# Moving four pieces of the mixer's query and gate work to GpSimd and ScalarE, and joining the first input transfers, in a two-layer decoder trunk

## The chip, the cores and the metric

The kernel runs on one core of a Trainium2 chip. The metric is the time of one launch in device microseconds (us); the median over repeated runs counts. The engines go by the names that the profile uses: PE is TensorE (matmuls), DVE is VectorE, ACT is ScalarE, POOL is GpSimd, SP is SyncE (its queue issues most of the transfers).

## What is computed

A trunk of two layers over 256 tokens of width 1024, in float32. Each layer is half a feed-forward block, three token mixers side by side, and another half feed-forward block:

```python
for l in range(DEPTH):
    x = x + 0.5 * swiglu_ffn(x, ffn1_norm[l], ffn1_w_gu[l], ffn1_w_down[l])
    h = rms_norm(x, mix_norm[l])
    x = x + hybrid_mixer(h, w_in[l], w_gate[l], ...)
    x = x + 0.5 * swiglu_ffn(x, ffn2_norm[l], ffn2_w_gu[l], ffn2_w_down[l])

# in the mixer (A: stick-breaking, B: NSA, C: DSA attention)
... = jnp.split(h @ w_in, offs, axis=-1)               # all queries, keys and values
qg = apply_rope(rms_norm(q, q_norm), cos, sin)         # B: 8 query heads of 64, the norm per head
kc = rms_norm(nsa_compress(k_cmp, ...), k_norm[0])     # B: compressed keys
g_a, g_b, g_c = jnp.split(jax.nn.sigmoid(h @ w_gate), 3, axis=-1)
merged = g_a * (o_a @ w_br_a) + g_b * (o_b @ w_br_b) + g_c * (o_c @ w_br_c)
return merged @ w_out
```

The kernel has the norm of `h` in two parts: the weights of the norm are multiplied into the matmul's input `aT`, and the token's reciprocal root mean square (`R`, one number for each token) is multiplied onto what the matmul gives.

## The kernel before

**Units.** All large products are made in units of 128 rows of weights by up to 1024 columns. For each unit the SP queue fetches the weights into one of four `raw` buffers; ACT copies them into `wh`, rounded to the matmul's reduced float type (L242); DVE subtracts, `wl = raw - wh` (L244); PE multiplies with both parts (L196) and adds up in a PSUM bank. `wh` and `wl` have three buffers each, and the program puts a unit's copy and subtraction two units ahead of its matmuls (`LA = 2`). So PE needs from DVE one subtraction of 128x1024 for each unit, on time.

**Threads between the units.** The small work of the mixer stands in Python generators. After each unit `tick()` lets each generator that is due go on to its next `yield n`, which means "again after n units". `keys` splits and transposes the keys, `compress` makes the compressed keys, `indexer` makes C's scores and picks keys by a chain of MAX8 and MATCH_REPLACE8 instructions on DVE, `queries` norms and rotates B's queries. The order of the matmuls is fixed by the program; for the other engines a scheduler sets an order that is then fixed, and each engine works through its own queue in that order.

**PSUM.** There are three banks with the tag `acc`, two with `tp` (for transposes on PE, L689) and two with `sc`. A third pair of transposes has to wait until the first has been copied out.

**The names at the change.** `gl` holds the gates' product with `R`: DVE reads the PSUM bank and `R` in one instruction of 128x512 (L624, `gate_rows`). `q8[0]` and `q8[1]` (tokens 0 to 127 and 128 to 255; `q8_402` and `q8_403` in the order below) hold the eight query heads, 128x512 each: multiplied by the norm `y` (L676) and by the norm's weights `hg` (L679), rotated (`ra`, `rb`, L648 to L652), then copied to a high part on ACT (L880) and subtracted for a low part on DVE (L881), and transposed on PE. `kD` is the transposed key of branch C, copied out of a `tp` bank by `evens` (L631), which takes ACT and DVE in turn. `dq` are C's queries; their transposes are copied out into `qD` (ACT, L795). `kC` is the transposed compressed key (ACT, L869). `hrep` is the compressor's hidden layer (DVE, L843), which PE multiplies by `w2` into the bank `o`. `p` copies on ACT (L526) take the key units' sums out of the `acc` banks. `dq<-p,dq`, `kk<-p,kk` and `kc<-p,kc` on POOL are low parts of keys and of C's queries (L700, L790), and `p<-c2s,cst` (L865) is a masked copy of the compressed values.

**The opening.** `x` comes in four transfers on SP's queue, each ahead of a unit's weights; the norms' weights `gn` (48 numbers for each partition) come by a transfer of their own from ACT's queue. ACT multiplies the first two blocks of `x` by `gn` (L375) and copies the first weights, and DVE makes the low parts.

## Time and profile before

| | |
|---|---|
| median of 3 runs | 1208.97 us (1208.77 to 1208.98) |
| the profiled execution: its time | 1211.23 us |
| the profiled execution: its span | 1209.5 us |
| PE busy | 1197.8 us, 99% of the span |
| PE's weight loads (beside the matmuls) | 1070.7 us, 89% |
| DVE busy | 884.2 us, 73% |
| ACT busy | 697.9 us, 58% |
| POOL busy | 145.8 us, 12% |

The span is the stretch on the chip from the first to the last instruction of the profile; the time of that execution holds 1.7 us more around it, and is 2.3 us over the median, so the profile's microseconds are used for differences and not for the whole. PE's 99% is busy time in which matmuls run on from one to the next; the 1% beside it is the start, the end and a few waits in the middle. The busy shares of the other engines are means over the whole span, and stretches of it differ a lot from these means.

### The profile page before, as it was taken

To read this page: it belongs to the slowest core of one execution; us is meant where nothing else is said; L and a number is where in the kernel's file an instruction comes from. 1 tells how busy PE (TensorE), PEld (TensorE's weight loads), DVE (VectorE), ACT (ScalarE), POOL (GpSimd) and SP (SyncE) were. 2 spreads that over 40 slices of the span, in tenths; PEclk is the share of its full clock that TensorE was granted. 3 is DMA by queue.
4 is the path that set the end of the run, shared out by engine and by line. 5 is a ranking of instruction groups with operands and counts; after the bars stand their busy time and mean duration, and the time that the engine had idled before them with its cause. 6 is when DMAs were issued, how large, how long until landed. Compare 5 with 4: busy or idle time off the path is not lost. (4 is left out here: it accounts for less than half of the span.)

```text
span 1209.5 us, 20859 instructions
## 1 busy us (share of the span) xinstructions
PE 1197.8 (99%) x7878; PEld 1070.7 (89%) x7878; DVE 884.2 (73%) x1577; ACT 697.9 (58%) x1261; POOL 145.8 (12%) x181
## 2 busy tenths in 40 slices
PE   8999999999999999999999999999999999999998
PEld 7888888879999988888888888898898999888887
DVE  7766677897766877776777666788977587876664
ACT  6655555565675565555555555555666745655542
POOL 2211011220000111110111110112100001111100
PEclk9999999999999999999999999999999999999999
DMA  7555566644334555556656555666533345555563
GB/s 263 187 185 184 179 190 200 216 152 136 122 95 152 180 189 190 190 187 190 191 181 192 189 182 184 188 188 219 166 123 113 106 155 187 191 192 192 183 200 106
DMA packets 60885, 212.09 MB, mean 175 GB/s; under 512 B 6992, under 2 KB 8048, under 8 KB 60784
## 3 DMA queue, kind: packets, MB, share of 16 engines
q1 hardware_dynamic: 60192, 209.65, 54.2%
q0 software_dynamic: 448, 1.08, 0.4%
q8 instruction: 62, 1.02, 0.3%
q14 instruction: 39, 0.32, 0.1%
q10 hardware_dynamic: 144, 0.02, 0.0%
HBM read 209.15 MB, written 1.05 MB: 174 GB/s over the span
## 5 line engine op out<-in xcount | busy, mean ns | idle before, releaser
L242 ACT ACTIVATE wh<-raw 128x1024 fp32r<-128x1024 f32 (+4 forms) x402 | 412.2, 1028 | 401.8 <-PE acc L196 277.8
L244 DVE TENSOR_TENSOR wl<-raw,wh 128x1024 fp32r<-128x1024 f32 (+4 forms) x400 | 473.9, 1187 | 211.5 <-ACT wh L242 210.6
L196 PE MATMUL acc<-aT,wh 128*128 128x512 f32 (+1 forms) x1696 | 415.1, 343 | 1.3 <-ACT wh L242 1.3
L196 PEld LDWEIGHTS acc<-aT,wh 128*128 128x128 f32 x1696 | 265.0, 189 | 41.9 <-ACT wh L242 1.7
L196 PE MATMUL acc<-aT,wl 128*128 128x256 f32 x1280 | 297.9, 281 | 1.2 <-DVE wl L244 1.2
L196 PE MATMUL acc<-hT,wh 128*128 128x512 f32 (+1 forms) x792 | 236.2, 367 | 0.0
L196 PEld LDWEIGHTS acc<-aT,wl 128*128 128x128 f32 x1280 | 216.1, 190 | 3.7 <-DVE wl L244 2.8
L196 PE MATMUL sc<-aT,wh 128*128 128x512 f32 x544 | 191.7, 396 | 0.0
L196 PE MATMUL acc<-hT,wl 128*128 128x256 f32 x704 | 184.5, 280 | 0.0
L196 PEld LDWEIGHTS acc<-hT,wh 128*128 128x128 f32 x792 | 137.2, 188 | 25.8
L196 PE MATMUL sc<-aT,wl 128*128 128x256 f32 x544 | 151.1, 279 | 0.0
L196 PEld LDWEIGHTS acc<-hT,wl 128*128 128x128 f32 x704 | 126.8, 188 | 0.0
L196 PEld LDWEIGHTS sc<-aT,wh 128*128 128x128 f32 x544 | 101.8, 188 | 24.0
L442 POOL TENSOR_TENSOR v<-v,R 128x256 f32<-128x256 f32 x88 | 70.6, 806 | 412.3 <-DVE v L358 359.2
L196 PEld LDWEIGHTS sc<-aT,wl 128*128 128x128 f32 x544 | 102.4, 188 | 0.4
L386 POOL TENSOR_TENSOR ssum<-ssum,sq 128x256 f32<-128x256 f32 x42 | 38.3, 912 | 445.5 <-ACT sq L385 445.3
L196 PE MATMUL acc<-wh,aT 128*128 128x512 f32 (+1 forms) x320 | 81.1, 394 | 0.2
L196 PEld LDWEIGHTS acc<-wh,aT 128*128 128x128 f32 x320 | 57.5, 188 | 11.0 <-ACT p L526 1.1
L357 ACT ACTIVATE half<-acc 128x256 f32<-128x256 f32 x136 | 49.5, 366 | 3.7 <-PE acc L196 3.2
L444 DVE TENSOR_TENSOR v<-v,v 128x256 f32<-128x256 f32 x88 | 38.2, 436 | 13.3 <-ACT v L443 5.8
L358 DVE TENSOR_TENSOR v<-acc,half 128x256 f32<-128x256 f32 x108 | 44.7, 417 | 1.5 <-ACT half L357 1.5
L376 DVE SCALAR_TENSOR_TENSOR aT<-x,gn,aT 128x256 fp32r<-128x256 f32 x48 | 40.6, 856 | 7.0 <-ACT aT L375 7.0
(239 smaller groups left out, 1217.2 us busy)
## 6 DMA issues: line engine op xcount, KB each, us to landing
raw<-in_gu SPq DMA_DIRECT2D x175, 512.0 KB, 4.0
raw<-in_dn SPq DMA_DIRECT2D x64, 512.0 KB, 3.7
raw<-in_wgate SPq DMA_DIRECT2D x48, 512.0 KB, 3.6
raw<-in_win SPq DMA_DIRECT2D x32, 512.0 KB, 3.7
raw<-in_dn SPq DMA_DIRECT2D x32, 384.0 KB, 3.0
raw<-in_wbr SPq DMA_DIRECT2D x16, 512.0 KB, 3.5
raw<-in_wout SPq DMA_DIRECT2D x16, 512.0 KB, 3.5
raw<-in_cw SPq DMA_DIRECT2D x8, 512.0 KB, 4.4
```

The lines of the kernel that those rows point to most:

```text
L196: return pe(T.matmul(o, lhsT=lhsT, rhs=rhs, start=start, stop=stop, skip_group_check=True))
L242: A.activation(out=wh[:, w], in_=raw[:, w], func=AF.Copy)
L244: e.tensor_tensor(out=wl[:, w], in0=raw[:, w], in1=wh[:, w].bitcast(F32), op=ALU.subtract)
L357: A.activation(out=t, in_=b[:, S:2 * S], func=AF.Copy)
L358: V.tensor_tensor(out=o, in0=b[:, 0:S], in1=t, op=ALU.add)
L376: V.scalar_tensor_tensor(out=dst[:, m, 1], in0=xs[m], scalar=g[:, m:m + 1], in1=dst[:, m, 0].bitcast(F32), op0=ALU.mult, op1=ALU.subtract)
L386: G.tensor_tensor(out=ssum, in0=ssum, in1=sq, op=ALU.add)
L442: G.tensor_tensor(out=g, in0=g, in1=N["R"], op=ALU.mult)
L444: V.tensor_tensor(out=u, in0=u, in1=g, op=ALU.mult)
```

## The change

Six edits, in two places of the program.

In the opening: `x` and the norms' weights lie in one array and one tile, `gn` in front. The first transfer of it (the weights and two blocks of `x`) is issued from ACT's queue, the transfer of `gn` alone is gone, and SP's queue begins with the first unit's weights.

In each layer's mixer:
- the first two of the six gate groups are copied from PSUM to `gl` by ACT, and the product with `R` is made in place by POOL (`scaled`, put off by 22 units); the other groups stay on DVE;
- the queries' product with `hg` is made by POOL (`nh == 8` are B's queries);
- the queries' low part is made by POOL;
- `kD` is always copied out by ACT;
- `compress` waits three units and not two before its product with `w2`.

```diff
--- before.py
+++ after.py
@@ -121,7 +121,7 @@
 
 
 @with_exitstack
-def decoder_trunk(ctx: ExitStack, tc: tile.TileContext, x_in, consts, gains, hgain, gu1, dn1, win, wkc, wgate, cw1, cw2,
+def decoder_trunk(ctx: ExitStack, tc: tile.TileContext, x_in, consts, hgain, gu1, dn1, win, wkc, wgate, cw1, cw2,
                   cpe, wbr, wout, gu2, dn2, out, depth=DEPTH):
     nc = tc.nc
     V, A, G, T = nc.vector, nc.scalar, nc.gpsimd, nc.tensor
@@ -154,15 +154,16 @@
     def cc(name):
         return cst[:, _C[name][0]:_C[name][1]]
 
-    xt_ = cpool.tile([P, KD, S], F32, tag="x", name="x")
-    xs = [xt_[:, m] for m in range(KD)]
-    gn = cpool.tile([P, DEPTH * 3, KD], F32, tag="gn", name="gn")
-    nc.scalar.dma_start(out=gn, in_=gains.rearrange("p (a k) -> p a k", k=KD))
-    xv = x_in.rearrange("p (k s) -> p k s", s=S)
+
+    NG = DEPTH * 3 * KD
+    xt_ = cpool.tile([P, NG + KD * S], F32, tag="x", name="x")
+    xs = [xt_[:, NG + m * S:NG + (m + 1) * S] for m in range(KD)]
+    gn = xt_[:, 0:NG].rearrange("p (a k) -> p a k", k=KD)
 
     first = [wpool.tile([P, D], F32, tag="raw", bufs=RAW, name=nm("raw")) for _ in range(KD // 2)]
     for u, w in enumerate(first):
-        nc.sync.dma_start(out=xt_[:, 2 * u:2 * u + 2], in_=xv[:, 2 * u:2 * u + 2])
+        k = slice(NG + 2 * u * S if u else 0, NG + 2 * (u + 1) * S)
+        (nc.sync if u else nc.scalar).dma_start(out=xt_[:, k], in_=x_in[:, k])
         n = D if u else D // 2
         for h in range(0, D, n):
             nc.sync.dma_start(out=w[:, h:h + n], in_=gu1[0][:, u * D + h:u * D + h + n])
@@ -621,10 +622,20 @@
                     return
                 if n % 2 == 0:
                     gl[n // 2] = b4("gl")
-                V.tensor_tensor(out=gl[n // 2][:, (n % 2) * 512:(n % 2 + 1) * 512].rearrange("p (a b) -> p a b", b=S),
-                                in0=gb[n].rearrange("p (a b) -> p a b", b=S),
-                                in1=N["R"].unsqueeze(1).to_broadcast([P, 2, S]), op=ALU.mult)
+                g = gl[n // 2][:, (n % 2) * 512:(n % 2 + 1) * 512].rearrange("p (a b) -> p a b", b=S)
+                b = gb[n].rearrange("p (a b) -> p a b", b=S)
+                r = N["R"].unsqueeze(1).to_broadcast([P, 2, S])
+                if n < 2:
+
+                    A.activation(out=g, in_=b, func=AF.Copy)
+                    spawn(scaled(g, r), 22)
+                else:
+                    V.tensor_tensor(out=g, in0=b, in1=r, op=ALU.mult)
             return f
+
+        def scaled(g, r):
+            G.tensor_tensor(out=g, in0=g, in1=r, op=ALU.mult)
+            yield 1
 
         turn = [0]
 
@@ -676,7 +687,8 @@
             V.tensor_tensor(out=v, in0=v, in1=r.unsqueeze(3).to_broadcast([P, nt, nh, HD]), op=ALU.mult)
             for a, n, k in gs:
                 g = hg[:, k * HD:(k + 1) * HD].unsqueeze(1).unsqueeze(1)
-                V.tensor_tensor(out=v[:, :, a:a + n], in0=v[:, :, a:a + n], in1=g.to_broadcast([P, nt, n, HD]),
+                e = G if nh == 8 else V
+                e.tensor_tensor(out=v[:, :, a:a + n], in0=v[:, :, a:a + n], in1=g.to_broadcast([P, nt, n, HD]),
                                 op=ALU.mult)
             yield 1
             rope(v, nh, 8, tab("cs")[:, t0:t0 + nt], tab("sn")[:, t0:t0 + nt])
@@ -784,7 +796,7 @@
                     A.activation(out=kSW[:, m, :, s], in_=heads(tp), func=AF.Copy)
                 yield 1
                 tp = transposes([k1[:, 0, 0:P], k1[:, 0, P:256]])
-                evens(out=kD[:, :, s], in_=heads(tp))
+                A.activation(out=kD[:, :, s], in_=heads(tp), func=AF.Copy)
             dq = b4("dq").rearrange("p (t h a d) -> p t h a d", t=NT, a=2, d=HD)
             A.activation(out=dq[:, :, :, 0].bitcast(F32R), in_=p1[:, :, 0:4], func=AF.Copy)
             G.tensor_tensor(out=dq[:, :, :, 1], in0=p1[:, :, 0:4], in1=dq[:, :, :, 0], op=ALU.subtract)
@@ -841,7 +853,7 @@
                 a, b = (v[:, kv * 2 * NC:(kv + 1) * 2 * NC].rearrange("p (g c) -> p g c", c=NC).unsqueeze(1)
                         .to_broadcast([P, 4, 2, NC]) for v in (hs, tp))
                 V.tensor_tensor(out=hrep[:, kv, :, :, 0:NC], in0=b, in1=a, op=ALU.mult)
-            yield 2
+            yield 3
             c2 = hid[:, S + P:2 * S]
             for kv in range(2):
                 mm(c2[:, kv * HD:(kv + 1) * HD], hrep[:, kv].rearrange("p i g c -> p (i g c)"), w2[:, kv], True, True)
@@ -878,7 +890,7 @@
             yield 2
             for t in range(NT):
                 A.activation(out=q8[t][:, :, 0:HD].bitcast(F32R), in_=q8[t][:, :, HD:P], func=AF.Copy)
-                V.tensor_tensor(out=q8[t][:, :, HD:P], in0=q8[t][:, :, HD:P], in1=q8[t][:, :, 0:HD], op=ALU.subtract)
+                G.tensor_tensor(out=q8[t][:, :, HD:P], in0=q8[t][:, :, HD:P], in1=q8[t][:, :, 0:HD], op=ALU.subtract)
             yield 2
             for t in range(NT):
                 for h in range(0, 8, 4):
@@ -1233,9 +1245,9 @@
     wbr = np.concatenate([i["w_br_a"], i["w_br_c"], wb], 1).reshape(L, KD, P, 4, S).transpose(0, 2, 3, 1, 4)
     wg = i["w_gate"].reshape(L, D, 3, 4, S)[:, :, ::-1].transpose(0, 1, 3, 2, 4).reshape(L, D, 3 * D)
     return {
-        "x": np.ascontiguousarray(i["x"].reshape(S, KD, P).transpose(2, 1, 0).reshape(P, KD * S)),
+        "x": np.concatenate([gains.transpose(2, 0, 1).reshape(P, -1),
+                             i["x"].reshape(S, KD, P).transpose(2, 1, 0).reshape(P, KD * S)], 1),
         "consts": _CONST,
-        "gains": np.ascontiguousarray(gains.transpose(2, 0, 1).reshape(P, -1)),
         "hgain": np.ascontiguousarray(hg),
         "gu1": gu1, "dn1": _tiles(i["ffn1_w_down"], [P] * KD),
         "win": _tiles(i["w_in"][:, :, _in_columns()], IN_G),
```

**The order at the queries, first layer.** On POOL, from the second pair of keys' low parts (`kk_562` before, `kk_560` now) to the last low part ahead of the next weights; `kc4_564` before is the compressed key (`kc4_569` now), and `p1_565` (`p1_570` now) is the masked copy of the compressed values. Before:

```order
L700 TENSOR_TENSOR kk_562_2862<-p1_401_2152,kk_562_2862 128x4x128
L700 TENSOR_TENSOR kc4_563_2865<-p1_401_2152,kc4_563_2865 128x128
L790 TENSOR_TENSOR dq_586_2990<-p1_401_2152,dq_586_2990 128x8x64
L865 TENSOR_TENSOR p1_565_2881<-c2s_532_2752,cst_70 128x512
L700 TENSOR_TENSOR kc4_564_2878<-c2s_532_2752,kc4_564_2878 128x128
```

Now:

```order
L712 TENSOR_TENSOR kk_560_2848<-p1_401_2150,kk_560_2848 128x4x128
L712 TENSOR_TENSOR kc4_561_2851<-p1_401_2150,kc4_561_2851 128x128
L802 TENSOR_TENSOR dq_586_2988<-p1_401_2150,dq_586_2988 128x8x64
L877 TENSOR_TENSOR p1_570_2920<-c2s_549_2804,cst_70 128x512
L637 TENSOR_TENSOR gl_503_2618<-gl_503_2618,R_454_2332 128x512
L691 TENSOR_TENSOR q8_402_2151<-q8_402_2151,hg_393_2137 128x8x64
L691 TENSOR_TENSOR q8_403_2152<-q8_403_2152,hg_393_2137 128x8x64
L893 TENSOR_TENSOR q8_402_2151<-q8_402_2151 128x8x64
L712 TENSOR_TENSOR kc4_569_2917<-c2s_549_2804,kc4_569_2917 128x128
L893 TENSOR_TENSOR q8_403_2152<-q8_403_2152 128x8x64
```

Between the masked copy and the compressed key's low part stand four new instructions of 128x512, the gate's product, the two halves of the queries times `hg`, and the first half's low part; the second half's low part stands behind.

On DVE in the same place. The `wl` are weights' subtractions, `isc` rows (the key choice) don't stand here, `w` and `y` belong to norms, `c2s`, `cra` and `crb` to the compressed key. Before, from the first half's product with `hg` to the copy of `kD`:

```order
L679 TENSOR_TENSOR q8_402_2153<-q8_402_2153,hg_393_2139 128x8x64
L860 TENSOR_TENSOR c2s_532_2752<-cra_555_2821,crb_556_2822 128x16
L663 SCALAR_TENSOR_TENSOR y_553_2812<-w_554_2813,y_553_2812 128x8
L648 TENSOR_TENSOR ra_578_2956<-q8_402_2153,cst_70 128x128
L676 TENSOR_TENSOR q8_403_2154<-q8_403_2154,y_553_2812 128x8x64
L649 TENSOR_TENSOR rb_579_2957<-q8_402_2153,cst_70 128x8x8
L679 TENSOR_TENSOR q8_403_2154<-q8_403_2154,hg_393_2139 128x8x64
L650 TENSOR_TENSOR rb_579_2957<-q8_402_2153,cst_70 128x8x8
L244 TENSOR_TENSOR wl_584_2971<-raw_582_2968,wh_583_2970 128x1024
L652 TENSOR_TENSOR q8_402_2153<-ra_578_2956,rb_579_2957 128x8x16
L637 CAST kD_414_2165<-tp_585_2986 128x2x128
```

Now, from the second half's product with the norm on:

```order
L687 TENSOR_TENSOR q8_403_2152<-q8_403_2152,y_547_2799 128x8x64
L674 SCALAR_TENSOR_TENSOR y_553_2810<-w_554_2811,y_553_2810 128x1
L245 TENSOR_TENSOR wl_573_2925<-raw_571_2922,wh_572_2924 128x1024
L867 SCALAR_TENSOR_TENSOR c2s_549_2804<-c2s_549_2804,y_553_2810,hg_393_2137 128x64
L659 TENSOR_TENSOR ra_578_2954<-q8_402_2151,cst_70 128x128
L869 TENSOR_TENSOR cra_562_2870<-c2s_549_2804,cst_70 128x16
L870 TENSOR_TENSOR crb_563_2871<-c2s_549_2804,cst_70 128x8
L871 TENSOR_TENSOR crb_563_2871<-c2s_549_2804,cst_70 128x8
L660 TENSOR_TENSOR rb_579_2955<-q8_402_2151,cst_70 128x8x8
L872 TENSOR_TENSOR c2s_549_2804<-cra_562_2870,crb_563_2871 128x16
L661 TENSOR_TENSOR rb_579_2955<-q8_402_2151,cst_70 128x8x8
L245 TENSOR_TENSOR wl_584_2969<-raw_582_2966,wh_583_2968 128x1024
```

The products with `hg` and the copy of `kD` are gone; both products with the norm stand ahead of the weights' subtraction `wl_573` and of the compressed key's rows, and the first half's rotation behind them. After these rows comes the last row of the first half's rotation (`q8_402<-ra_578,rb_579`), as before.

**The order at the transposes, first layer.** On ACT; `wh` are copies of weights, `tp_585` holds `kD`'s transposes, `tp_592` those of C's first queries. Before, from the compressed key's high part on:

```order
L699 ACTIVATE kc4_564_2878<-c2s_532_2752 128x128
L880 ACTIVATE q8_402_2153<-q8_402_2153 128x8x64
L242 ACTIVATE wh_595_3029<-raw_594_3027 128x1024
L795 ACTIVATE qD_412_2163<-tp_592_3017 128x4x128
L869 ACTIVATE kC_415_2166<-tp_593_3023 128x64
L880 ACTIVATE q8_403_2154<-q8_403_2154 128x8x64
L242 ACTIVATE wh_601_3068<-raw_600_3066 128x1024
```

Now, from the first half's high part on:

```order
L892 ACTIVATE q8_402_2151<-q8_402_2151 128x8x64
L243 ACTIVATE wh_590_2999<-raw_589_2997 128x1024
L711 ACTIVATE kc4_569_2917<-c2s_549_2804 128x128
L799 ACTIVATE kD_414_2163<-tp_585_2984 128x2x128
L892 ACTIVATE q8_403_2152<-q8_403_2152 128x8x64
L243 ACTIVATE wh_594_3023<-raw_593_3021 128x1024
L807 ACTIVATE qD_412_2161<-tp_592_3015 128x4x128
L243 ACTIVATE wh_601_3066<-raw_600_3064 128x1024
```

The copy of `kD` is new on ACT and stands behind the queries' first high part, a copy of weights and the compressed key's high part; the copy to `qD` comes after the second half's high part and another copy of weights; the copy to `kC` has gone further back.

On PE in the same place; `tp` rows are transposes, `acc` rows a unit's matmuls. Before:

```order
L689 MATMUL tp_592_3017<-cst_70,dq_586_2990 128x128 x4
L689 MATMUL tp_593_3023<-cst_70,kc4_564_2878 128x128 x2
L196 MATMUL acc_574_2930<-wh_583_2970,aT_8_143 128x512 x2
L196 MATMUL acc_575_2931<-wh_583_2970,aT_8_143 128x512 x2
L196 MATMUL acc_574_2930<-wh_583_2970,aT_8_143 128x512 x2
L196 MATMUL acc_575_2931<-wh_583_2970,aT_8_143 128x512 x2
L196 MATMUL acc_574_2930<-wl_584_2971,aT_8_143 128x512 x2
L196 MATMUL acc_575_2931<-wl_584_2971,aT_8_143 128x512 x2
L689 MATMUL tp_597_3050<-cst_70,dq_586_2990 128x128 x4
L196 MATMUL acc_603_3072<-wh_590_3001,aT_8_143 128x512 x2
```

Now:

```order
L701 MATMUL tp_592_3015<-cst_70,dq_586_2988 128x128 x4
L197 MATMUL acc_574_2928<-wh_583_2968,aT_8_141 128x512 x2
L197 MATMUL acc_575_2929<-wh_583_2968,aT_8_141 128x512 x2
L197 MATMUL acc_574_2928<-wh_583_2968,aT_8_141 128x512 x2
L197 MATMUL acc_575_2929<-wh_583_2968,aT_8_141 128x512 x2
L197 MATMUL acc_574_2928<-wl_584_2969,aT_8_141 128x512 x2
L197 MATMUL acc_575_2929<-wl_584_2969,aT_8_141 128x512 x2
L701 MATMUL tp_596_3044<-cst_70,dq_586_2988 128x128 x4
L701 MATMUL tp_599_3060<-cst_70,kc4_569_2917 128x128 x2
L197 MATMUL acc_603_3070<-wh_590_2999,aT_8_141 128x512 x2
```

The compressed key's transposes (from `kc4_564` before, from `kc4_569` now) have moved from right behind the first transposes of `dq` to right behind the second ones. The `tp` bank of the second ones is that of `kD`'s transposes, and the bank of the compressed key's that of the first ones of `dq`.

## Rows read from the trace of the kernel before

**Rows 1.** The page's first part: busy time of each engine, its share of the span, and its instructions.
```profile
PE 1197.8 (99%) x7878; PEld 1070.7 (89%) x7878; DVE 884.2 (73%) x1577; ACT 697.9 (58%) x1261; POOL 145.8 (12%) x181
```

**Rows 2.** PE's waits over the whole span: what PE waited with, for what, then us in total, times, longest us.
```profile
PE tp L689 <- DVE kD L637: 2.9, 2, 1.5
PE acc L196 <- ACT wh L242: 1.3, 1, 1.3
...
PE o L196 <- ACT wh L242: 0.7, 1, 0.7
```

**Rows 3.** Busy time of each engine in two stretches, one in each layer, from the mixer's key units to its query transposes.
```profile
245.00:278.00 33.00, 30.72 (x177) 26.36 (x178) 33.00 (x99) 21.26 (x41) 5.97 (x6) 1.00 0.47 147
842.00:876.00 34.00, 32.44 (x185) 27.45 (x185) 34.00 (x102) 21.73 (x42) 6.32 (x6) 1.00 0.47 149
```

**Rows 4.** PE's timeline in the first layer: start, duration, engine, line, operation, out<-in, tiles, and in brackets the idle time ahead and what ended it.
```profile
243.92 1.07 PE L196 MATMUL acc<-wl,aT 128*128 128x512 f32 x4
245.68 0.63 PE L196 MATMUL o<-w,hrep 128*128 128x64 f32 x4 [0.70 <-ACT wh L242]
...
265.17 0.60 PE L689 MATMUL tp<-cst,dq 128*128 128x128 f32 x4
267.24 0.41 PE L689 MATMUL tp<-cst,kc 128*128 128x128 f32 x2 [1.47 <-DVE kD L637]
267.40 2.08 PE L196 MATMUL acc<-wh,aT 128*128 128x512 f32 x8
269.32 1.07 PE L196 MATMUL acc<-wl,aT 128*128 128x512 f32 x4
270.24 0.60 PE L689 MATMUL tp<-cst,dq 128*128 128x128 f32 x4
270.59 2.48 PE L196 MATMUL acc<-wh,aT 128*128 128x512 f32 x8
272.90 1.07 PE L196 MATMUL acc<-wl,aT 128*128 128x512 f32 x4
```

**Rows 5.** The same of the second layer.
```profile
862.54 0.60 PE L689 MATMUL tp<-cst,dq 128*128 128x128 f32 x4
864.60 0.41 PE L689 MATMUL tp<-cst,kc 128*128 128x128 f32 x2 [1.46 <-DVE kD L637]
...
867.98 2.47 PE L196 MATMUL acc<-wh,aT 128*128 128x512 f32 x8
```

**Rows 6.** DVE's timeline in the first layer.
```profile
245.31 0.27 DVE L843 TENSOR_TENSOR hrep<-o,hs 128x120 f32<-128x120 f32 x1
...
255.02 1.25 DVE L244 TENSOR_TENSOR wl<-raw,wh 128x1024 fp32r<-128x1024 f32 x1
...
256.26 1.26 DVE L657 TENSOR_SCALAR u<-hs 128x8 f32<-128x8 f32 x2
...
258.62 0.67 DVE L624 TENSOR_TENSOR gl<-acc,R 128x512 f32<-128x512 f32 x1
...
261.72 0.68 DVE L676 TENSOR_TENSOR q<-q,y 128x512 f32<-128x512 f32 x1
...
262.64 0.68 DVE L679 TENSOR_TENSOR q<-q,hg 128x512 f32<-128x512 f32 x1
...
264.34 0.95 DVE L679 TENSOR_TENSOR q<-q,hg 128x512 f32<-128x512 f32 x1
...
265.35 1.21 DVE L244 TENSOR_TENSOR wl<-raw,wh 128x1024 fp32r<-128x1024 f32 x1
266.48 0.28 DVE L652 TENSOR_TENSOR q<-ra,rb 128x128 f32<-128x128 f32 x1
266.68 0.41 DVE L637 CAST kD<-tp 128x256 fp32r<-128x256 f32 x1
...
269.96 1.28 DVE L881 TENSOR_TENSOR q<-q 128x512 f32<-128x512 f32 x2
```

**Rows 7.** POOL's timeline in the first layer.
```profile
253.07 1.30 POOL L700 TENSOR_TENSOR kk<-p,kk 128x512 f32<-128x512 f32 x1 [7.96 <-ACT kk L699]
...
255.24 2.18 POOL L790 TENSOR_TENSOR dq<-p,dq 128x512 f32<-128x512 f32 x1
257.50 1.05 POOL L865 TENSOR_TENSOR p<-c2s,cst 128x512 f32<-128x512 f32 x1
263.88 0.86 POOL L700 TENSOR_TENSOR kc<-c2s,kc 128x128 f32<-128x128 f32 x1 [5.33 <-ACT kc L699]
```

**Rows 8.** ACT's timeline in the first layer.
```profile
266.79 0.63 ACT L880 ACTIVATE q<-q 128x512 fp32r<-128x512 f32 x1 [2.99 <-DVE q L652]
267.33 1.04 ACT L242 ACTIVATE wh<-raw 128x1024 fp32r<-128x1024 f32 x1
268.27 0.58 ACT L795 ACTIVATE qD<-tp 128x512 fp32r<-128x512 f32 x1
...
270.54 0.46 ACT L526 ACTIVATE p<-acc,rq 128x256 f32<-128x256 f32 x1
```

**Rows 9.** The opening, all engines and queues (ACTq is ACT's queue, where transfers are issued).
```profile
0.74 0.41 ACTq L160 DMA_DIRECT2D gn<-in_gains  x1
...
5.60 0.91 ACT L375 ACTIVATE aT<-x,gn 128x256 fp32r<-128x256 f32 x2 [2.93 <-DMA gn<-in_gains]
...
6.87 0.72 PE L196 MATMUL acc<-aT,wh 128*128 128x512 f32 x2 [1.29 <-ACT wh L242]
```

## The prediction

> **What bounds the kernel now.** I read the page's first part, then PE's waits, then the two stretches that the change touches, and in these the timelines of the four engines.
>
> PE is busy for 99% of the span [rows 1]. So work taken off another engine is worth something only where PE waits for it. The list of PE's waits is short: 2.9 us in two waits for DVE's copy of `kD`, 0.7 us put down to ACT ahead of the product with `hrep`, and 1.3 us at the opening [rows 2]. The edits in the mixer can win from the first two and the few tenths beside them, no more.
>
> Why do these waits exist? In the stretch from the key units to the queries' transposes DVE is busy for 33.00 of 33.00 us in the first layer and for 34.00 of 34.00 in the second, while ACT has 21.26 and POOL 5.97 [rows 3]. There the queue of DVE sets the time, against 73% in the mean. I measure PE's waits as start minus start, since the modelled ends run into the next row:
>
> - `hrep`, first layer only: four `acc<-wl` matmuls take 0.92 (269.32 to 270.24), from 243.92 to 245.68 it is 1.76: 0.84 lost [rows 4]. It is put down to ACT, but DVE ends `hrep` at 245.58 (245.31 + 0.27) [rows 6], 0.1 ahead of PE's start: it waits for DVE.
> - The transposes of `kc`: transposes of `dq` take 0.35 (270.24 to 270.59), from 265.17 to 267.24 it is 2.07: 1.72 lost. In the second layer, 862.54 to 864.60, 1.71 [rows 4, 5]. DVE starts the copy of `kD` at 266.68 [rows 6] in a queue behind products, rotation and weights.
> - Eight `acc<-wh` matmuls last 2.48 in place of 2.08 (2.47 against 2.10 there): 0.40 and 0.37 lost [rows 4, 5]. ACT's `p` copies, which begin at 270.54 [rows 8], free a bank in their middle.
>
> Together 2.96 in the first layer and 2.08 in the second, 5.04 in all.
>
> **What DVE and POOL do to each other.** The same `q<-q,hg` on DVE takes 0.68 at 262.64 and 0.95 at 264.34 [rows 6]; from 263.88 to 264.74 POOL was at `kc` [rows 7]. Two `u` of 128x8 take 1.26 [rows 6] and end at 257.52, 0.10 after POOL's `dq` (255.24 + 2.18 = 257.42) [rows 7]. And `dq` has 2.18 where `kk` of the same size has 1.30 [rows 7]. So they hold each other up, each until the other's instruction ends, and an instruction put on POOL holds back DVE's next one that is touched by this. The chip's behaviour here decides the case.
>
> [...] By the whole of a `kk` as the block, the sum below would be some 0.9 us higher.
>
> **The change, part by part.** POOL gets six instructions of 128x512 in a layer. Price of one: from 1.05 (`p<-c2s,cst`) over 1.30 (`kk`) to 2.18 (`dq`) as elapsed time [rows 7]; once DVE lets go, `dq` ran from about 256.27 (the end of the weights' subtraction, 255.02 + 1.25 [rows 6]) to 257.42: 1.15. I take 1.15, since these too will start out of such a wait.
>
> DVE gives up, by spacing of starts: two `gl` of 0.60, two `q<-q,hg` of 0.60 and up, two low parts of 0.60 (1.28 for two), one `kD` of 0.34 [rows 6]. Of the first `gl` and the low parts nothing counts ahead of the rotation.
>
> [...]
>
> *The waits that go.* `compress` asks for `hrep` one unit later, some 2.8 us (267.40 to 270.24 is a unit [rows 4]), and DVE has it by 245.6: the 0.84 are won. The transposes of `kc` no longer need the bank of `kD`: the 1.7 go from there, but the second transposes of `dq` now need that bank, and those of `kc` the bank of the first ones.
>
> *First layer and second, on the clock of rows 4 to 8.* DVE has no idle time, so rows taken out bring on what follows, and blocks push it back.
>
> 1. First product with the norm, 261.72 before [rows 6]. Out ahead of it: `gl` 0.60, the weights' subtraction 1.13 (265.35 to 266.48), the block in `u` 1.1 (1.26 less the 0.14 or so that they need), and 0.7 for the compressed key's small rows and a MATCH_REPLACE that now stand behind (an estimate from durations of 0.07 to 0.4). In: the second half's small rows 0.2, and three blocks: `dq` 0.7, the masked copy 0.7, `gl` 0.9. These are 1.15, 1.05 and 1.15 less the 0.3 to 0.45 in which DVE has rows of the key choice, which are not held up. So 261.72 - 3.53 + 2.5 = 260.7.
> 2. The two products follow each other, 260.7 to 262.0. Then POOL's first product with `hg` holds until 263.15, and the weights' subtraction `wl_573` ends at 264.4. PE wants it at 265.17 - 0.92 = 264.25 [rows 4], in the first layer at 263.4 since 0.84 were won: waits of 1.0 and 0.15.
> 3. POOL's second product, 264.35 to 265.5, holds DVE for 1.1. Then the first half's rotation and the compressed key's rows, 1.0, the subtraction `wl_584`, 1.13, and the last row, 0.28: 267.9. Before it was 266.48 + 0.28 = 266.76.
> 4. ACT: high part 0.54 (266.79 to 267.33), weights 0.94 (267.33 to 268.27) [rows 8], the compressed key 0.25, `kD` 0.41 as on DVE [rows 6]: 270.05. PE wants the second transposes of `dq` 0.35 + 2.84 after the first, which now start near 265.35: 268.55. Wait 1.5, in both layers.
> 5. ACT: second high part, weights, `qD` (0.58 [rows 8]): 272.1. PE wants the transposes of `kc` at 270.45: wait 1.7.
> 6. ACT: weights and two `p` copies: 273.8. PE wants the bank some 0.6 after the transposes of `kc`, at 272.75: wait 1.05, where 0.4 were.
>
> Sum: 1.0 + 1.5 + 1.7 + 1.05 = 5.25 in the first layer, 0.15 + 4.25 = 4.4 in the second: 9.65 against 5.04, so +4.6 us.
>
> The first queries' transposes come 3.6 us after that (272.90 to 276.54 before), and the last low part on POOL ends some 2 us ahead of them: no term. The gates' products are wanted after 290 us: none either; without this cover the POOL price of 1.15 each.
>
> *The opening.* ACT starts `aT` at 5.60 when `gn` lands, and PE starts at 6.87 after the copy of weights [rows 9]. With `gn` in the same transfer as `x` and the weights asked for first, the two land together as before or some tenths to either side: 0, with 0.6 to both sides.
>
> Forecast: 1208.97 + 4.6 + 0 = 1213.6 us (the median; differences carry over, the profiled execution's own 1211.23 would become 1215.8).
>
> **Rivals.**
> - *Late, but absorbed (as before).* The waits 4 to 6 come from one lateness of some 2.3 us a layer: each microsecond that the first rotation is earlier takes one from the sum of its layer. If DVE is held up by only half of what I put (the blocks fall on rows of the key choice, which are let through; step 2 and 3 hold 4.5 of blocks), the sum is again 5 and the time 1209, within 2 either way. For it: the scheduler's order has such rows at hand. Against it: behind both products with the norm stands none of them.
> - *POOL doesn't hold DVE up.* Then the rotation is 4.5 earlier, `hrep` and `kD` cost nothing and only the 0.4 stay: 5.04 - 0.77 = 4.3 won, 1204.7 us. It decides from the point where `kD`'s copy ends before 268.55. Against it: the 0.95 and the 1.26 above.
> - *POOL's price is that of `dq`.* Three products in the chain with 1.0 more each, in two layers: +6, 1219.6 us. For it: 2.18 is in the rows. Against it: that time holds a wait for DVE which I have counted.
> - *The mixer's edits are neutral and only the opening shows:* 1208.4 to 1209.6; it falls in with the first rival.
>
> **How the numbers follow.** The forecast's case has 0.50, its own range is 1211.3 to 1217 (prices 1.05 to 1.30, opening 0.6, step 1 uncertain by 0.5 a layer). Absorbed: 0.25. No holding up: 0.17. `dq`'s price: 0.08. The range, 1205 to 1218, leaves out the last and about half of the third, 0.17. What counts as no change is 0.2%, 2.4 us, so 1206.6 to 1211.4. Faster: 0.17 + 0.04 of the absorbed. Same: 0.19 of the absorbed, 0.03 of the forecast's. Slower: 0.47 + 0.02 + 0.08.
>
> **What would show it.** In the list of PE's waits: `hrep` gone; `tp` waiting for ACT at the second transposes of `dq` and at `kc`, 1.5 and 1.7 in each layer. On DVE, rows of 1.2 to 1.8 us just behind the two products with the norm, that end with POOL's. On POOL, products with `hg` of 1.15 to 2. On ACT, the first high part at 267 to 268, later than 266.79. Wrong if DVE runs on at 0.68 beside POOL, or if ACT copies `kD` ahead of the high part's wait: then the forecast falls to a rival. A new wait outside these stretches is nowhere in my sum.

## The result, and the profile after

The changed kernel takes 1219.17 us (median, 1215.11 to 1219.24) against 1208.87 us before: ratio 1.0081, 95% interval 1.0068 to 1.0093. It is slower, as forecast, but by 10 us and not by 4.6, and outside the range of 1205 to 1218. The profiled executions are 1211.23 us before and 1219.24 us after, 8.0 apart; what the other 2 may be is told in the last section.

The page's first part: the span has grown from 1209.5 to 1217.5 us, PE's busy time only by 4.9 [rows 1].

```profile
PE 1202.7 (99%) x7878; PEld 1074.3 (88%) x7878; DVE 887.5 (73%) x1563; ACT 699.2 (57%) x1267; POOL 166.7 (14%) x193
```

PE's waits over the whole span (waited with, for what; us in total, times, longest):

```profile
PE tp L701 <- ACT qD L807: 3.1, 2, 1.6
PE tp L701 <- ACT kD L799: 2.2, 2, 1.1
PE acc L197 <- DVE wl L245: 1.7, 3, 0.8
PE acc L197 <- ACT p L527: 1.5, 2, 0.8
```

The wait for `kD` on DVE and the one ahead of `hrep` [rows 2] are gone; in their place PE waits for the copies of `qD` and `kD` on ACT and for a bank that ACT's `p` copies free. PE's timeline in the first layer (start, duration, ..., in brackets the idle time ahead and what ended it), to be read against [rows 4]:

```profile
247.52 0.56 PE L197 MATMUL o<-w,hrep 128*128 128x64 f32 x4
...
262.98 1.19 PE L197 MATMUL acc<-wl,aT 128*128 128x512 f32 x4 [0.43 <-DVE wl L245]
...
266.30 1.08 PE L197 MATMUL acc<-wl,aT 128*128 128x512 f32 x4
268.47 0.66 PE L701 MATMUL tp<-cst,dq 128*128 128x128 f32 x4 [1.09 <-ACT kD L799]
270.70 0.44 PE L701 MATMUL tp<-cst,kc 128*128 128x128 f32 x2 [1.57 <-ACT qD L807]
270.90 0.70 PE L197 MATMUL acc<-wh,aT 128*128 128x512 f32 x2
272.38 2.92 PE L197 MATMUL acc<-wh,aT 128*128 128x512 f32 x6 [0.78 <-ACT p L527]
275.10 1.42 PE L197 MATMUL acc<-wl,aT 128*128 128x512 f32 x4
```

And in the second [rows 5]:

```profile
864.64 1.20 PE L197 MATMUL acc<-wl,aT 128*128 128x512 f32 x4 [0.47 <-DVE wl L245]
...
870.14 0.66 PE L701 MATMUL tp<-cst,dq 128*128 128x128 f32 x4 [1.09 <-ACT kD L799]
872.37 0.44 PE L701 MATMUL tp<-cst,kc 128*128 128x128 f32 x2 [1.57 <-ACT qD L807]
...
874.04 2.93 PE L197 MATMUL acc<-wh,aT 128*128 128x512 f32 x6 [0.77 <-ACT p L527]
```

By starts, as the prediction measured it, the first layer loses 0.6 for the weights' low part `wl`, 1.25 at the second transposes of `dq` (268.47 - 266.30 - 0.92), 1.88 at those of `kc` (270.70 - 268.47 - 0.35) and 1.0 at the bank (272.38 - 270.90 - 0.47 for two matmuls): 4.7. The second layer has 0.6, 1.26, 1.88 and 1.0. Together 9.5 against 5.04 before: +4.4.

Then something that was not in my sum. Six `acc<-wh` matmuls from 272.38 to 275.10 take 2.72, where eight took 1.92 before (267.40 to 269.32 in [rows 4]). Busy time in six stretches, for PE, PE's weight loads, DVE, ACT and POOL, and behind these five the granted clock:

```profile
267.00:271.00 4.00, 1.34 (x9) 0.72 (x8) 4.00 (x12) 3.83 (x8) 3.43 (x3) 1.00 0.43 131
273.00:275.00 2.00, 2.00 (x6) 1.62 (x5) 1.97 (x9) 0.65 (x3) 0.00 (x0) 0.50 0.49 102
275.50:276.00 0.50, 0.50 (x3) 0.43 (x2) 0.40 (x1) 0.50 (x1) 0.00 (x0) 0.67 0.82 336
...
870.00:872.00 2.00, 0.66 (x4) 0.42 (x4) 2.00 (x7) 1.83 (x4) 1.52 (x3) 1.00 0.32 129
874.00:879.00 5.00, 4.96 (x12) 3.89 (x13) 3.76 (x10) 2.38 (x5) 0.00 (x0) 0.50 0.63 177
880.00:881.00 1.00, 1.00 (x5) 0.81 (x5) 0.00 (x0) 0.00 (x0) 0.00 (x0) 1.00 0.52 193
```

Up to 271 us in the first layer and 872 us in the second the granted clock is 1.00, while PE works for 1.34 of the 4 us from 267 and for 0.66 of the 2 us from 870. By the end of the last wait it falls to 0.50 and stays there until about 275.8 and 880.0. The loss by starts: 2.72 - 1.44 and 1.25 - 0.92 in the first layer (the next row starts at 276.35), 1.6 us; in the second from 874.04 until the clock is back, against the same matmuls before, 2.8 us. Together 4.4. So the 8.0 are, to 0.1, 4.4 of waits + 4.4 of low clock - 0.7 won at the opening.

How the lateness arises, in the first layer, DVE first:

```profile
259.92 0.68 DVE L687 TENSOR_TENSOR q<-q,y 128x512 f32<-128x512 f32 x1
260.52 1.27 DVE L674 SCALAR_TENSOR_TENSOR y<-w,y 128x1 f32<-128x1 f32 x1
...
262.85 1.30 DVE L867 SCALAR_TENSOR_TENSOR c2s<-c2s,y,hg 128x64 f32<-128x64 f32 x1
...
266.00 0.28 DVE L663 TENSOR_TENSOR q<-ra,rb 128x128 f32<-128x128 f32 x1
...
267.27 1.22 DVE L663 TENSOR_TENSOR q<-ra,rb 128x128 f32<-128x128 f32 x1
```

POOL in the same time:

```profile
257.51 1.32 POOL L637 TENSOR_TENSOR gl<-gl,R 128x512 f32<-128x512 f32 x1
260.00 4.06 POOL L691 TENSOR_TENSOR q<-q,hg 128x512 f32<-128x512 f32 x2 [1.18 <-DVE w L673]
267.08 1.27 POOL L893 TENSOR_TENSOR q<-q 128x512 f32<-128x512 f32 x1 [3.02 <-ACT q L892]
```

`y<-w,y` of 128x1 takes 1.27 and `c2s<-c2s` of 128x64 takes 1.30; without POOL beside them the same rows take 0.15 and 0.28 (in the run with the products back on VectorE, below). They lie beside POOL's two products with `hg` (260.00 to 264.06), and `c2s` ends 0.1 after the second. The last row of the second half's rotation (267.27) takes 1.22, and POOL's low part runs from 267.08 to 268.35. The first half's rotation ends at 266.28; between the end of the products with the norm (260.52) and that lie 5.8 us. ACT's queue, which waits for it:

```profile
266.38 0.63 ACT L892 ACTIVATE q<-q 128x512 fp32r<-128x512 f32 x1 [7.36 <-DVE q L663]
...
268.06 0.36 ACT L799 ACTIVATE kD<-tp 128x256 fp32r<-128x256 f32 x1
...
270.07 0.58 ACT L807 ACTIVATE qD<-tp 128x512 fp32r<-128x512 f32 x1
...
271.50 0.46 ACT L527 ACTIVATE p<-acc,rq 128x256 f32<-128x256 f32 x1
```

ACT has stood idle for 7.36 us at the high part, and everything stands behind it: `kD`, whose transposes PE had done by 260.7, is copied at 268.06, `qD` at 270.07, the first `p` at 271.50.

The opening [rows 9]: PE's first real matmul starts at 5.99 and not at 6.87, since `aT` starts at 4.92.

```profile
4.92 0.89 ACT L376 ACTIVATE aT<-x 128x256 fp32r<-128x256 f32 x2
...
5.99 0.90 PE L197 MATMUL acc<-aT,wh 128*128 128x512 f32 x2
```

### The profile page after: what moved, and what is told of

Its sections match the earlier page's. It is cut to its first block, busy times and chain, and to the rows that moved or that the text cites. A ratio compares the mean times of both kernels' runs of the same rounds, so it can differ in the third digit from the quotient of the medians.

```text
span 1217.5 us, 20873 instructions
## 1 busy us (share of the span) xinstructions
PE 1202.7 (99%) x7878; PEld 1074.3 (88%) x7878; DVE 887.5 (73%) x1563; ACT 699.2 (57%) x1267; POOL 166.7 (14%) x193
## 3 DMA queue, kind: packets, MB, share of 16 engines
HBM read 209.15 MB, written 1.05 MB: 173 GB/s over the span
## 4 chain that ended last, share of the span: by engine, by line
PE 91%; DVE 5%; ACT 1%; POOL 1%; issue 1%; DMA 0%; SPq 0%; DVEq 0%; ACTq 0%; POOLq 0%
PE acc L197 70%; PE sc L197 17%; PE tp L701 2%; PE o L197 2%; DVE wl L245 2%; ACT wh L243 1%; POOL ssum L387 1%; DMA raw<-in_gu 0%; DVE isc L770 0%; DVE y L674 0%; PE tp L197 0%; DVE m L769 0%; POOL v L443 0%; DVE c2s L867 0%; DVE hs L684 0%
## 5 line engine op out<-in xcount | busy, mean ns | idle before, releaser
L197 PE MATMUL acc<-wh,aT 128*128 128x512 f32 (+1 forms) x320 | 84.1, 405 | 1.5 <-ACT p L527 1.5
L502 ACT ACTIVATE E<-sc,mx 128x128 f32<-128x128 f32 (+1 forms) x80 | 32.6, 418 | 21.6 <-DVE mx L917 21.5
```

The source lines that it names most:

```text
L197: return pe(T.matmul(o, lhsT=lhsT, rhs=rhs, start=start, stop=stop, skip_group_check=True))
L502: e = A.activation(func=func, **kw)
```

## The experiments

Theory A: POOL's instructions hold DVE up, the first rotation is late, and PE feels it through ACT's queue, in which the copies that PE needs stand behind the waiting high copy; what comes on top is the clock. Rivals: DVE's lost time itself sets the end (B); the new place of the transposes and of `kD` costs (C). All comparisons are with the kernel before on the same chip; its medians there were 1209.10, 1207.76 and 1209.37 us.

**The changed kernel again**, on the chip of the second group of runs, unchanged.

> The changed kernel itself, on the same chip as the three others of this call and as the kernel before. If the loss is in the two mixers (waits, then the low clock), it is again 8 us like for like in the traces; the medians may differ from that by the pace of the first feed-forward block's matmuls, which the traces so far show at 0.353 or at 0.347 us for a pair, in one kernel too (about 1.9 us for each block).

1217.53 us against 1207.76, ratio 1.0079 (1.0064 to 1.0094). The loss repeats. The trace has the same waits for `kD` and `qD`, the wait for a bank in the first layer only, and a granted clock of 0.84 on the mean from 262 to 284 us and from 862 to 884 us.

**ScalarE's order turned round.**

```diff
+ kd_ins.append(A.activation(out=kD[:, :, s], in_=heads(tp), func=AF.Copy))
...
+ qd_ins.append(A.activation(out=qD[:, :, t * P:(t + 1) * P], in_=heads(tp), func=AF.Copy))
...
- A.activation(out=q8[t][:, :, 0:HD].bitcast(F32R), in_=q8[t][:, :, HD:P], func=AF.Copy)
+ hi = A.activation(out=q8[t][:, :, 0:HD].bitcast(F32R), in_=q8[t][:, :, HD:P], func=AF.Copy)
+ nosync(hi, (qd_ins or kd_ins)[-1])
```

`nosync(a, b)` makes the scheduler put `a` behind `b`, without a semaphore; `...` stands for lines left out.

> The changed kernel with one thing turned round on ScalarE: the queries' high copies stand behind the copies of kD and qD and not ahead of them (an order between instructions of one engine; the work is the same, and VectorE's and GpSimd's queues are nearly the same). Theory A (GpSimd's products hold VectorE up, the first rotation is late, and PE only feels it because the copies of kD and qD and the p copies stand behind the waiting high copy in ScalarE's queue): the waits of 1.25, 1.81 and 0.94 us a layer shrink to at most 0.5 together, the wait of 0.6 for the weights' low part stays, the granted clock stays at 1.00 behind it: 1219.2 - 7 - 4.4 = about 1207, 1205 to 1209. Rival B (VectorE's lost time itself sets the end, whatever ScalarE's order): within 2 us of 1219. Rival C (the new place of the key transposes on PE is to blame): the transposes still wait for over 1 us each, 1215 or more.

1209.48 us, ratio 1.0002 (0.9992 to 1.0012): the whole loss is gone by the order of one engine alone, with all four pieces of work still where the change put them. ACT's timeline:

```profile
265.10 0.37 ACT L802 ACTIVATE kD<-tp 128x256 fp32r<-128x256 f32 x1
...
266.31 0.59 ACT L810 ACTIVATE qD<-tp 128x512 fp32r<-128x512 f32 x1
...
269.64 1.19 ACT L896 ACTIVATE q<-q 128x512 fp32r<-128x512 f32 x2
```

`kD` is copied at 265.10, `qD` at 266.31, the high copies at 269.64. The three waits are gone but for 0.4 at the bank, the clock is 1.00. DVE is held up as before:

```profile
260.49 1.27 DVE L674 SCALAR_TENSOR_TENSOR y<-w,y 128x1 f32<-128x1 f32 x1
...
262.82 1.30 DVE L870 SCALAR_TENSOR_TENSOR c2s<-c2s,y,hg 128x64 f32<-128x64 f32 x1
```

So B and C fall. The time is 0.5 us over the range given; now the queries' transposes are late, a wait that was not foreseen:

```profile
PE tp L701 <- DVE qN L648: 1.8, 2, 0.9
```

**Only kD ahead of the high copies.**

```diff
- A.activation(out=kD[:, :, s], in_=heads(tp), func=AF.Copy)
+ kd_ins.append(A.activation(out=kD[:, :, s], in_=heads(tp), func=AF.Copy))
...
- A.activation(out=q8[t][:, :, 0:HD].bitcast(F32R), in_=q8[t][:, :, HD:P], func=AF.Copy)
+ hi = A.activation(out=q8[t][:, :, 0:HD].bitcast(F32R), in_=q8[t][:, :, HD:P], func=AF.Copy)
+ nosync(hi, kd_ins[-1])
```

> The changed kernel with only the copy of kD ahead of the queries' high copies on ScalarE; qD and the p copies still stand behind them. Theory A: the wait of 1.25 us at the second transposes of dq goes to 0, but qD is as late as before, so the wait at kc's transposes grows from 1.8 to about 3.1: the sum a layer stays at 4.6 and the time at 1219, 1 us to either side. Rival (the copy of kD on ScalarE is the cause by itself): 2.5 us less or better, 1216.7 or below.

1217.25 us, ratio 1.0065 (1.005 to 1.008). PE's timeline:

```profile
268.71 0.44 PE L701 MATMUL tp<-cst,kc 128*128 128x128 f32 x2 [3.16 <-ACT qD L809]
```

The second transposes of `dq` come without a wait, and those of `kc` wait 3.16 us: the wait has moved, as theory A has it, and the granted clock falls as before, to 0.84 on the mean from 262 to 284 us and from 862 to 884 us. The time lies between the two forecasts (1218 at the least by theory A, 1216.7 at the most by the rival), so the place of the wait decides and not the time. This trace also has the quicker pace of the last section in its first block, worth 1.8 us by the estimate there; without it the time would be 1219. Here one late instruction at the head of a queue costs once, wherever the first of its followers is wanted.

**The products with hg back on VectorE.**

```diff
- e = G if nh == 8 else V
+ e = V
```

> The changed kernel with only the queries' products with their norm weights back on VectorE (0.6 us each there). Theory A: the two blocks of 1.2 us behind the products with the norm are gone and 1.2 us of own work come in, the first rotation is 1.1 us earlier, the wait for kD's copy goes to 0, kc's to 0.9, the bank's stays near 1.0: 2.1 us less a layer, and some or all of the clock's loss of 4.4: 1210.6 to 1215. Rival (GpSimd doesn't hold VectorE up at all): the products' 1.2 us on VectorE make it later, 1219 or above.

1210.78 us, ratio 1.0012 (1.0002 to 1.0021), in the range of theory A. DVE's timeline, to be read against that of the changed kernel:

```profile
258.26 0.15 DVE L674 SCALAR_TENSOR_TENSOR y<-w,y 128x1 f32<-128x1 f32 x1
...
258.93 0.28 DVE L867 SCALAR_TENSOR_TENSOR c2s<-c2s,y,hg 128x64 f32<-128x64 f32 x1
259.13 0.68 DVE L691 TENSOR_TENSOR q<-q,hg 128x512 f32<-128x512 f32 x1
...
262.80 0.28 DVE L663 TENSOR_TENSOR q<-ra,rb 128x128 f32<-128x128 f32 x1
```

`y<-w,y` takes 0.15 and `c2s<-c2s` 0.28 where they took 1.27 and 1.30, and from the end of the products with the norm (258.26) to the end of the first rotation (263.08) it is now 4.8 us, 0.9 less than there, though DVE does 1.2 us more of its own work. The clock stays at 1.00 (262 to 284 and 862 to 884 us). The longest wait left is one for POOL's low part of the compressed key, which stands behind the queries' first low part:

```profile
PE tp L701 <- POOL kc L712: 2.3, 2, 1.1
```

**The waits filled.**

```diff
+ def fill(n):
+     fb = psum("sc", SC)
+     for _ in range(n):
+         mm(fb[:, 0:P], warm, warm, True, True)
...
+ if t == 1:
+     fill(11)
...
+ fill(16)
  tp = transposes([kc4[:, 0, 0:P], kc4[:, 0, P:256]])
+ fill(8)
```

> The changed kernel with matmuls of no use (128x128, bf16, on a tile of zeros) put on PE where it waits: 11 ahead of the second transposes of dq, 16 ahead of kc's transposes, 8 behind these, so that PE is busy in most of what were the three waits; nothing else moves. Theory A with the clock as the second half of the loss (granted clock 0.87 in 265 to 275 us and 0.66 in 870 to 880, matmuls at half speed behind the waits): the waits end at the same times, the granted clock stays near 1.00, and the time falls by the loss of 1.6 + 2.8 us, to about 1215. Rival (the low clock has another cause, or costs nothing): 1219 or above.

1213.03 us, ratio 1.0032 (1.0021 to 1.0043), 2 us under the forecast. The matmuls of no use run in the waits. Counted from the first transposes of `dq`, the three waits end after 4.45, 6.70 and 8.37 us, in the changed kernel after 4.46, 6.69 and 8.37: they are as long as before. But the six `acc<-wh` matmuls behind them take 1.66 and not 2.92:

```profile
267.36 1.06 PE L197 MATMUL sc<-warm 128*128 128x128 bf16 x16
...
270.79 1.66 PE L197 MATMUL acc<-wh,aT 128*128 128x512 f32 x6 [0.27 <-ACT p L527]
```

The two mixers' stretches, the granted clock again behind the five engines:

```profile
262.00:284.00 22.00, 20.59 (x136) 17.16 (x135) 17.52 (x47) 11.49 (x19) 6.62 (x5) 1.00 0.57 171
862.00:884.00 22.00, 20.58 (x136) 17.12 (x135) 17.47 (x47) 11.49 (x19) 6.46 (x5) 1.00 0.59 173
```

The granted clock is 1.00 in both stretches. In this trace the span is 1211.3 us, 1.8 over that of the kernel before. Ahead of the three waits it is 1.6 us earlier than the changed kernel (the first `dq` transposes start at 262.42 and not at 264.01), which I put down to the quicker pace in the first layer's first block (last section, where the pace is worth 1.8 by estimate): 3.6 like for like, against 8.0 of the changed kernel. That is 4.4 us less, the loss read from the clock. So half of the change's cost in the traces was the clock, and it fell because PE stood idle in the waits.

**The opening alone.** The kernel before with the first, second and last piece of the diff.

> The kernel before with only the opening's edit. In the changed kernel's trace PE's first real matmul starts 0.88 us earlier and 0.7 of it are left at 38 us. If the mixer's edits are the whole of the loss, this alone gives 0.7 us: 1208.3, 1207 to 1209.5. Rival (nothing of it reaches the end, as predicted): 1209.0.

1207.61 us, ratio 0.9995 (0.9985 to 1.0004): no difference that can be told. In the trace 0.6 us are won at 38 us. Its first layer also has no wait ahead of `hrep` and 0.54 us at the transposes of `kc`, where the trace of the kernel before has 0.84 and 1.72: 2.0 us less, and why isn't settled.

**Gates alone on GpSimd.** The changed kernel with the products and the low parts on DVE.

```diff
- e = G if nh == 8 else V
+ e = V
- G.tensor_tensor(out=q8[t][:, :, HD:P], ...
+ V.tensor_tensor(out=q8[t][:, :, HD:P], ...
```

> The changed kernel with the queries' products and their low parts back on VectorE; the gate's products stay on GpSimd, kD on ScalarE, the later step of the compressor and the opening stay. Theory A (GpSimd and VectorE hold each other up; the compressed key's low part on GpSimd waits behind the queries' first low part): against the version with the products alone on VectorE the wait of 1.1 us at kc's transposes goes too, some 2 us in two layers, the rest stays: 1208 to 1209.5. Rival (the low parts on GpSimd cost nothing, since they are wanted late): no change against that version, 1210.8.

1208.81 us, ratio 1.0009 (0.9999 to 1.0019). The wait at `kc` for POOL is gone, as expected, and the time is in theory A's range. But the kernel before is 1.3 us faster on this chip than on that of the version with the products alone on VectorE, and the two ratios are 1.0009 and 1.0012: the 2 us that theory A saw in the low parts aren't shown by the times, and the rival isn't excluded.

**Nothing new on GpSimd.** The kernel with the opening's edit, `kD` on ACT and the compressor's later step.

> The kernel before with the opening's edit, kD always on ScalarE and the compressor's later step; nothing new on GpSimd, the gates as before on VectorE. Theory A (all that was lost comes from work on GpSimd that holds VectorE up): the waits for hrep and for kD go, some 1 us a layer of waits for the weights' low part, for qD and for a bank stays, no low clock: 1206.5, 1205 to 1208. Rival C (the new place of the transposes on PE and of kD on ScalarE costs by itself): 1209 or above.

1206.90 us, ratio 0.9990 (0.9981 to 1.0000), as theory A had it. The waits left in the mixers:

```profile
PE acc L197 <- ACT p L527: 1.5, 2, 0.8
...
PE tp L691 <- ACT qD L797: 0.3, 1, 0.3
```

The new place of `kD` and of the transposes costs nothing by itself; C falls a second time.

**The products alone on GpSimd, and the low parts alone,** each added to the version above.

> The version without new work on GpSimd (opening, kD on ScalarE, later step of the compressor) with the queries' products with their norm weights alone on GpSimd. Theory A: two blocks of 1.2 us on VectorE for 1.2 us of own work, the scheduler puts the waiting high copy ahead of kD again; waits of about 0.4 (weights), 0 to 0.5 (kD), 1.8 (qD) and 1.0 (bank) a layer, 2 us more than without: 1211 to 1213, up to 1215 if the clock falls. Rival (the products alone are harmless, it takes all three pieces on GpSimd): 1207.

1210.06 us, ratio 1.0007 (0.9997 to 1.0016): dearer than without by 0.0017, about 2 us, half of what theory A had at the least, and under its range. In the profiled execution the waits are 1.0 for `qD` and 0.75 for a bank in each layer, and the clock stays at 1.00 in both mixers. Four of the ten executions, though, have a mean granted clock of 0.998 over the whole span, the others 0.999 or 1.000 and the changed kernel 0.994 to 0.996: in these four it may have fallen for a short time.

> The version without new work on GpSimd, with the queries' low parts alone on GpSimd. Theory A: the first low part holds up the last row of the second half's rotation by about 1.0 us, and with it the second high copy and qD: 1 us a layer, 1208 to 1209.5. Rival (the low parts are wanted late and cost nothing): 1206.9, 0.7 to either side.

1207.93 us, ratio 0.9985 (0.9976 to 0.9995). In microseconds this lies between the two forecasts, but the kernel before is 1.6 us slower on this chip than on that of the version without new work; by the ratios, 0.9985 against 0.9990, the rival was right: by themselves the low parts cost nothing that can be told.

**The best of these,** the version without new work on GpSimd, with ACT's order turned round as above.

> The version without new work on GpSimd, with the queries' high copies behind the copies of kD and qD and the p copies on ScalarE. Theory A (the waits left, 0.3 for qD and 0.8 for a bank a layer, come from the waiting high copies): both go, the queries' transposes are still in time: 1.5 us less, 1205.4, 1204.5 to 1206.5. Rival (the low parts are then late for the queries' transposes, as in the version with the turned order, where PE waited 0.9 us for a query bank): 1207 or above.

1206.86 us against 1209.37, ratio 0.9980 (0.9971 to 0.9990): 2.5 us faster than the kernel before and, by the ratios, about 12 faster than the change. The waits for `qD` and the bank (1.8 us) are gone as expected, but 1.6 us are back at the queries' transposes, as the rival had it:

```profile
PE tp L691 <- DVE q L886: 1.6, 2, 0.9
```

The time lies between the two forecasts. That this version is faster than the one without the turned order (0.9990) isn't shown, since the two intervals overlap.

## Why the prediction was wrong

**Right, with sizes.** The list of waits and their places. `hrep` comes without a wait (247.52). The weights' low part: forecast 1.0 and 0.15, measured 0.6 and 0.6. Second transposes of `dq`: 1.5, measured 1.25. Those of `kc`: 1.7, measured 1.88. The bank: 1.05, measured 1.0. In all +4.6 forecast and +4.4 measured; that the sums agree to 0.2 is partly luck, since the terms are off by -0.4 to +0.45. The steps under them too: the products with the norm end at 260.52, and two blocks of 1.2 us on DVE follow (steps 2 and 3), the compressed key's row and the small row of its norm. The first high part on ACT starts at 266.38 and not at 267 to 268, but PE's first transposes of `dq` are early as well (264.01, forecast 265.35), so its lateness against PE is 2.4 us where the forecast had 2.6. The queue on ACT is the one of steps 4 to 6, and the runs with that queue's order changed show that it is the way by which the lateness gets to PE. That a POOL instruction holds a DVE instruction up until it ends is seen in `c2s<-c2s`, 1.30 beside POOL's product and 0.28 without it.

**The step that failed** is the sum itself, "so +4.6 us": it counted PE's idle time as the whole price of the waits. With 4.7 us of waits within 12 us the granted clock fell to 0.50 by their end, and the matmuls behind them, up to about 275.8 and 880.0, cost 1.6 and 2.8 us more. The run with the waits filled gave these 4.4 us back. The profile of before could not show it, since its clock is 1.00 in both mixers; its waits, 2.96 us in the first layer, did not bring it down, and neither did the waits of 1.0 and 0.75 in the profiled execution with the products alone. The prediction named the waits with their lengths and never asked what PE's clock does in them. With 4.4 us more for the clock and 0.7 less for the opening, the forecast of 1213.6 would be 1217.3; the 1.9 us from there to 1219.17 stay open (last section). Ahead of the 0.50 at 273 and 874 us PE was idle only in pieces, the longest 1.88 us; how much idle time it takes for the clock to fall isn't shown.

**The opening** was put at 0, within 0.6. It is 0.7 won at 38 us in this trace; alone, its time can't be told from no change.

**The rivals.** Absorption did not come: the blocks did not fall on rows of the key choice, which was its condition, but on `y` and `c2s`. (Rows of the key choice do run on beside POOL: in the trace of before two MATCH_REPLACE take 0.27 and 0.40 us at 257.51 and 257.77, beside the masked copy from 257.50 to 258.55, as they do at 250.08 and 249.69 without it.) "POOL doesn't hold DVE up" falls by `y` and `c2s` too. "POOL's price is that of `dq`" gives 1219.6 us, next to the measured time, but by coincidence: it puts all of the loss into waits, of which the trace has 4.4 us more than before, and POOL's price did not rise to that of `dq` as such, since the gate's product took 1.32 and the two products 4.06 together with the waits for DVE before and between them.

**More than the parts.** Against the version with nothing new on POOL the gates alone cost 0.0019 of the time, the products alone 0.0017, the low parts alone nothing; all three together 0.0089. Each ratio is known to about 0.001 to either side, and the products and the low parts alone ran on another chip than the rest. The parts make one chain late, and ACT's queue passes it on. In the traces the clock is low in the mixers only with all three parts on POOL (the changed kernel's two, with 0.84 to 0.92 on the mean of the 22 us, and the one with only `kD` ahead, with 0.84). Two parts at a time were run only as gates and low parts, so what the products would cost with one of the others isn't shown.

## What to carry to other kernels

Before an instruction is moved from VectorE to GpSimd, look at what VectorE does beside it: where it is full, small instructions there stood still until GpSimd's ended (1.27 and 1.30 us, 0.15 and 0.28 without it), and 1.2 us of work moved away came back as two blocks of 1.2 us. Look also at the queue that waits for the moved work: a copy that is ready stands behind one that isn't, and here turning two places in ScalarE's queue took back all that the change had lost. And price a wait of TensorE twice where several come close together: as idle time, and as the low clock on the matmuls behind it (here 4.4 us each).

## What the runs showed of the hardware beside that

In the stretch of the first feed-forward block the matmuls run at one of two paces, at a granted clock of 1.00 either way, and one kernel has both in different executions. Busy times in 70 us of each layer's first block, the profiled execution of the kernel before:

```profile
60.00:130.00 70.00, 70.00 (x397) 60.69 (x397) 47.78 (x76) 40.48 (x74) 9.61 (x13) 1.00 0.58 183
660.00:730.00 70.00, 70.00 (x397) 60.65 (x397) 48.08 (x74) 40.46 (x75) 9.38 (x13) 1.00 0.58 186
```

And that of the version with only `kD` ahead of the high copies, which has the same code there:

```profile
60.00:130.00 70.00, 70.00 (x406) 61.72 (x405) 48.73 (x76) 41.59 (x76) 9.57 (x13) 1.00 0.64 187
660.00:730.00 70.00, 70.00 (x398) 60.74 (x397) 47.97 (x75) 40.23 (x74) 9.52 (x13) 1.00 0.63 184
```

PE is never idle in any of them, and does 397 or 398 matmuls in three of the stretches and 406 in the fourth, 2% more; over a block that is about 1.8 us, an estimate from these counts. The changed kernel has 398 in the first layer in one profiled execution and 406 in the other. Executions of one kernel lie up to 3 or 4 us apart (the kernel before: 1206.89 to 1210.35 in 25 runs), and the pace can make up 1.8 of that for each block. So a part of the 10 us between the medians, beyond the 8.0 between two traces that have the slower pace in both layers, may be this; it isn't shown. A second candidate is the profiled execution of the kernel before: at 1211.23 us it is slower than all others on record, and the trace with the opening alone, whose mixers have the same code, has 2.0 us less of waits in its first layer. What sets the pace is open; no run was made for it.
